# Differential attention in a hybrid encoder layer: the second half of each attention step is queued by a count of TensorE columns

## The chip, the cores and the metric

The kernel runs on one core of a Trainium2 chip. The metric is the device time of one execution in microseconds. Three runs of the kernel before gave 915.10, 917.85 and 918.49 us; the median is 917.85 us. One more execution was recorded by the hardware profiler; that execution took 916.89 us, and the span of its trace, from first to last instruction, is 915.0 us. All durations here come from that trace.

## The reference

One encoder layer over 512 tokens of width 1024, in float32. The part that the change touches is the attention branch: 8 heads, each with two softmax maps over 64-wide queries and keys, and values of 128 columns.

```python
q = apply_rope(rms_norm(q, q_norm_gain[l]), cos, sin)
k = apply_rope(rms_norm(k, k_norm_gain[l]), cos, sin)
# for one block of 128 queries:
s = jnp.einsum('bqhcd,bkhcd->bhcqk', q_blk, k) * scale       # c: the two maps
p = jax.nn.softmax(s, axis=-1)
p_diff = p[:, :, 0] - lam * p[:, :, 1]
o = jnp.einsum('bhqk,bkhd->bqhd', p_diff, v)
# then per head: o = rms_norm(o, attn_subln_gain) * (1 - lam_init), and the output projection
```

Around it stand an RG-LRU branch ahead of attention, the gates and output projections behind it, and a mixture of 16 experts that takes the last third of the time.

## The kernel before, in words

**Precision.** Every large product is made of three: each operand is split into a high part (a cast on ScalarE, L186) and a low part (a subtraction on VectorE, L187), and high x high, high x low and low x high are added in PSUM. So each weight tile that a projection uses costs ScalarE and VectorE one instruction each.

**The attention stage** runs over four pairs of heads (`for j in range(4)`, L735), and in each over eight steps: two heads `hh` times four blocks `t` of 128 queries. A step has three parts:

- `scores` (L617): for each of the two maps two TensorE products of 512 columns into the tile `sps`, a row maximum on VectorE (L630, into `mx`), and an exponential on ScalarE (L631, into `ee`, with the row sum by a second, accumulator-reading instruction).
- `apply_v` (L635): two tiny VectorE instructions on `mx` (L638, L639), then one of 512 columns that makes `ee` the difference of the two maps (L640); four TensorE transposes of `ee` into `pps` (L643); ScalarE casts `pps` to the high part of `PT` (L186), VectorE subtracts to get the low part (L187).
- `outputs` (L647), put into a list `held` by `apply_v`: four products with the high part of `PT` and four with the low part into `ops` (L651), a copy on ScalarE (L653) and an addition on VectorE (L654). After a head's last step, `finish_head` (L660) normalizes the head (L666 to L670) and puts its own transposes, `turn` (L672), into `held`.

**Work beside the steps.** So that TensorE has something to do while ScalarE and VectorE make a step's softmax, chunks of other work are put beside the steps (list `beside`): for pairs 0 to 2 the query/key projections of the next pair (`qk_tok`, four chunks of 24 products of 512 columns, with L559 on ScalarE, L560 to L572 on VectorE and L182, L574, L575 on GpSimd behind each), its value projections (`v_half`, two chunks of 48 products of 256 columns), the stacking of queries and keys (`stack`), and gate chunks of 24 products (`gate_pieces`). Pair 3 has gate chunks only.

**What sets the order.** The Python code gives the program order. `held` is a list of [columns, function]; each projection and each `scores` calls `go_on` (L360) after a group of products, which takes the group's columns off every entry and runs those that reach zero, behind that group on TensorE. On each engine the instructions are then put into a fixed order ahead of time by a scheduler of the language, which keeps program order as priority and lets an instruction pass others where it takes those for not yet ready. On the chip each engine works through its own list in order and waits on semaphores.

In the loop of L753, step `n` first does all but the last of its chunks, then the scores of step `n + 1`, then `apply_v` of step `n`, then its last chunk:

```python
for p_ in beside[n][:-1]: p_()
if n + 1 < len(steps): sm[n + 1] = scores(pr, *steps[n + 1])
apply_v(pr, hh, t, *sm.pop(n))
for p_ in beside[n][-1:]: p_()
```

Of the kernel before, what the change touches and what calls it, by code (L numbers as in the profile page):

```python
# [24 lines left out]
NH = 8  # L25
# [13 lines left out]
BEHIND = 29  # L39
FIRST = 3  # L40
HEAD = 18000
WARM = 20
BETWEEN = (4, 4, 2)
VALUES = 2500
# [58 lines left out]
def _bc(ap, axis, n):  # L103
    a = ap.unsqueeze(axis)
    shape = list(a.shape)
    shape[axis] = n
    return a.broadcast_to(shape)
# [3 lines left out]
def hybrid_layer(ctx, tc, x, w_in, w_ao, w_lo, w_out, w_lg, w_rt, w_eg, w_eu, w_ed, pp, rw, cst, out):  # L111
# [4 lines left out]
    def f(ap):  # L116
        return ap.bitcast(F32)
# [12 lines left out]
    def pss(name):  # L130
        return psp.tile([P, 512], F32, tag="S", name=name, bufs=3)

    def pm(name, dt=F32):
        return psp.tile([P, 512], dt, tag="M", name=name, bufs=3)
# [23 lines left out]
    def unit(tag, shape, dt, name):  # L158
        pool, n = places[tag]
        return pool.tile(shape, dt, tag=tag, name=name, bufs=n)  # L160
# [9 lines left out]
    def keep_busy(n, behind=None):  # L170

        with ExitStack() as order:
            if behind is not None:
                order.enter_context(tc.issue_after(behind))
            for _ in range(n):
                mm(idle_ps, idle[:, 0:P], idle, start=True, stop=True)

    keep_busy(WARM)

    def rpow(dst, src):  # L180
        n = src.free_size()
        return POOL.tensor_tensor(dst, src, mhalf[:, :n], op=ALU.pow)  # L182


    def split(dst_hi, dst_lo, src, eng=DVE):
        i_ = ACT.copy(dst_hi, src)  # L186
        return i_.ins, eng.tensor_tensor(dst_lo, src, f(dst_hi), op=ALU.subtract).ins  # L187
# [167 lines left out]
    held = []  # L355
# [4 lines left out]
    def go_on(last, n):  # L360

        for h in held:
            h[0] -= n
        due = [h for h in held if h[0] <= 0]
        for h in due:
            held.remove(h)
            with tc.issue_after(last.ins):
                h[1]()
# [222 lines left out]
    def stack(pr, hh, qi):  # L591


        j = pr.j
        ps = pm(f"tps{qi}{j}{hh}")
        for t in range(NT):
            PE.transpose(ps[:, t * P:(t + 1) * P], pr.qr[qi][:, t, hh * P:(hh + 1) * P], ident)
        names = ("q",) if qi == 0 else ("k0", "k1")
        st = [unit(n, [P, 2, S], F32R, f"st_{n}{j}{hh}") for n in names]
        for s in range(2):  # L600
            own, oth = slice(64 * s, 64 * s + 64), slice(64 - 64 * s, 128 - 64 * s)
            a = st[0][:, s]
            ACT.copy(a[own], ps[own])
            DVE.tensor_tensor(a[oth], ps[own], f(a[own]), op=ALU.subtract)
            pr.st[hh, qi, s, 0] = a
            if qi:
                b = st[1][:, s]
                ACT.copy(b[oth], ps[own])
                DVE.tensor_copy(b[own], a[oth])
                pr.st[hh, qi, s, 1] = b  # L610

    def new_pair(j):
        pr = Pair()
        pr.j, pr.qr, pr.st, pr.s0s, pr.on = j, {}, {}, {}, {}
        return pr

    def scores(pr, hh, t):  # L617
        h = 2 * pr.j + hh
        if t == 0:
            pr.s0s[hh] = at.tile([P, NT], F32, tag="s0s", name=f"s0s{h}", bufs=2)  # L620
            pr.on[hh] = at.tile([P, NT, P], F32, tag="on", name=f"on{h}", bufs=2)
        mx = at.tile([P, 6], F32, tag="mx", name=f"mx{h}{t}", bufs=3)
        ee = unit("ee", [P, 2, S], F32, f"ee{h}{t}")
        for c in range(2):
            ps = pss(f"sps{h}{t}{c}")
            q = pr.st[hh, 0, c, 0][:, t * P:(t + 1) * P]
            mm(ps, q, pr.st[hh, 1, c, 0], start=True, stop=False)
            l = mm(ps, q, pr.st[hh, 1, c, 1], start=False, stop=True)  # L628
            go_on(l, 2 * 512)
            DVE.tensor_reduce(mx[:, c:c + 1], ps, axis=AX.X, op=ALU.max, negate=True)  # L630
            ACT.activation(ee[:, c], ps, AF.Exp, bias=mx[:, c:c + 1],  # L631
                           accum_out=(pr.s0s[hh][:, t:t + 1] if c == 0 else mx[:, 3:4]))
        return mx, ee

    def apply_v(pr, hh, t, mx, ee):  # L635

        h = 2 * pr.j + hh
        DVE.reciprocal(mx[:, 4:5], mx[:, 3:4])  # L638
        DVE.scalar_tensor_tensor(mx[:, 5:6], pr.s0s[hh][:, t:t + 1], NEGLAM, mx[:, 4:5], op0=ALU.mult, op1=ALU.mult)  # L639
        DVE.scalar_tensor_tensor(ee[:, 0], ee[:, 1], mx[:, 5:6], ee[:, 0], op0=ALU.mult, op1=ALU.add)  # L640
        pt = pm(f"pps{h}{t}")
        for kb in range(NT):
            PE.transpose(pt[:, kb * P:(kb + 1) * P], ee[:, 0, kb * P:(kb + 1) * P], ident)  # L643
        PT = unit("PT", [P, 2, S], F32R, f"PT{h}_{t}")
        split(PT[:, 0], PT[:, 1], pt)

        def outputs():  # L647
            po = pm(f"ops{h}{t}")
            for i in range(2):
                for kb in range(NT):  # L650
                    mm(po[:, 0:256], PT[:, i, kb * P:(kb + 1) * P], pr.vhl[kb // 2][:, kb % 2, hh],  # L651
                       start=(kb == 0 and i == 0), stop=(kb == NT - 1 and i == 1))
            ACT.copy(pr.on[hh][:, t], po[:, P:256])  # L653
            DVE.tensor_tensor(pr.on[hh][:, t], pr.on[hh][:, t], po[:, 0:P], op=ALU.add)  # L654
            if t == NT - 1:
                finish_head(pr, hh)

        held.append([VALUES, outputs])

    def finish_head(pr, hh):  # L660
        h = 2 * pr.j + hh
        on, s0s = pr.on[hh], pr.s0s[hh]
        so = at.tile([P, 3, NT], F32, tag="so", name=f"so{h}", bufs=2)
        sj = at.tile([P, P], BF16, tag="sj", name=f"sj{h}")
        for t in range(NT):
            ACT.activation(sj, on[:, t], AF.Square, accum_out=so[:, 0, t:t + 1])  # L666
        DVE.scalar_tensor_tensor(so[:, 1], s0s, P * EPS, s0s, op0=ALU.mult, op1=ALU.mult)
        DVE.tensor_tensor(so[:, 1], so[:, 1], so[:, 0], op=ALU.add)
        rpow(so[:, 2], so[:, 1])
        POOL.tensor_tensor(on, on, _bc(so[:, 2], 2, P), op=ALU.mult)  # L670

        def turn():  # L672
            pt = pm(f"otp{h}")
            for t in range(NT):
                PE.transpose(pt[:, t * P:(t + 1) * P], on[:, t], ident)
            if pr.j < 3:
                ACT.activation(oT[pr.j][:, hh], pt, AF.Copy, scale=subg)
            else:
                hi, lo = new_o(h)
                ACT.activation(hi, pt, AF.Copy, scale=subg)  # L680
                DVE.scalar_tensor_tensor(lo, pt, subg, f(hi), op0=ALU.mult, op1=ALU.subtract)

        held.append([HEAD, turn])

    oS = {}

    def new_o(h):

        o = unit(("qr", "qr", "va", "vb", "q", "k0", "k1", "ee")[h], [P, 2, S], F32R, f"o{h}")
        oS[h] = o[:, 0], o[:, 1]  # L690
        return oS[h]

    def split_o(h):
        split(*new_o(h), oT[h // 2][:, h % 2])

    def pieces(pr):
        return [lambda t=t: qk_tok(pr, t) for t in range(NT)] + \
               [lambda tp=tp: v_half(pr, tp) for tp in range(2)]
# [16 lines left out]
    pr = new_pair(0)  # L715
# [19 lines left out]
    for j in range(4):  # L735
        nxt = new_pair(j + 1) if j < 3 else None
        beside = [[] for _ in range(2 * NT)]
        beside[0] += [lambda: stack(pr, 1, 0), lambda: stack(pr, 1, 1)]
        if nxt:
            for n, p_ in zip((0, 1, 2, 3, 5, 6), pieces(nxt)):  # L740
                beside[n].append(p_)
            beside[5].append(lambda: stack(nxt, 0, 0))
            beside[6].append(lambda: stack(nxt, 0, 1))
            for n in GATES[j]:
                beside[n].append(gates.pop(0))
        else:
            for n, h in ((2, 0), (2, 1), (3, 2), (4, 3), (5, 4), (6, 5)):
                beside[n].append(lambda h=h: split_o(h))
            for n in GATES[j]:
                beside[n].append(gates.pop(0))  # L750
        steps = [(hh, t) for hh in range(2) for t in range(NT)]
        sm = {0: scores(pr, *steps[0])}
        for n, (hh, t) in enumerate(steps):  # L753
            for p_ in beside[n][:-1]:
                p_()
            if n + 1 < len(steps):
                sm[n + 1] = scores(pr, *steps[n + 1])
            apply_v(pr, hh, t, *sm.pop(n))
            for p_ in beside[n][-1:]:
                p_()  # L760
        pr = nxt


# [115 lines left out]
    pr = pss("rank")  # L879
# [427 lines left out]
```

## Time and profile before

| what | us |
|---|---|
| median of three runs | 917.85 |
| the profiled execution | 916.89 |
| its span | 915.0 |
| TensorE busy in the span | 878.4 |
| VectorE busy | 696.6 |
| ScalarE busy | 589.8 |
| GpSimd busy | 219.1 |
| attention stage, first scores to last chunk | about 255 to 494 in the span |

In the profile, PE is TensorE's products, PEld its weight loads, DVE VectorE, ACT ScalarE, POOL GpSimd. A name such as `sps` is the program's tile without its number; L643 is a line of the kernel. A product of 512 columns is shown with a modelled length of 0.39 us, while such products start 0.23 us apart, so a busy TensorE is judged by starts, not by lengths.

### The profile page before, as it was taken

How to read it: one execution, taken by the hardware profiler on the slowest of the kernel's cores; microseconds unless marked ns; L12 is line 12 of the kernel's file. 1: busy time of each engine (PE TensorE's matmuls, PEld its weight loads, DVE VectorE, ACT ScalarE, POOL GpSimd, SP SyncE). 2: the span in 40 equal slices, each digit the busy share in tenths (PEclk: the TensorE clock that was granted, in tenths of full speed). 3: DMA queues.
4: the chain of work that ended last, by engine and by line, in shares of the span. 5: the costliest groups of instructions: out<-in, count | busy, mean ns of one | idle time of the engine just before them, and what ended most of it. 6: DMA issues, size and time to landing. Idle time of an engine off the chain costs nothing. (4 is left out here: it accounts for less than half of the span.)

```text
span 915.0 us, 12610 instructions
## 1 busy us (share of the span) xinstructions
PE 878.4 (96%) x4504; PEld 700.1 (77%) x4504; DVE 696.6 (76%) x1091; ACT 589.8 (64%) x917; POOL 219.1 (24%) x215
## 2 busy tenths in 40 slices
PE   8999999999999999999999999969999999999993
PEld 5887787788878978878888878947777777777772
DVE  5558977864389689887895653579999999999982
ACT  6698887533255565765784323338888888888881
POOL 6600000080027027056110001432312311121010
PEclk9999999999999999999999999979999999999997
DMA  6621422323312222203236277589999999999952
GB/s 228 211 92 47 138 80 82 93 92 116 92 46 71 51 64 69 70 1 116 93 104 242 92 246 246 179 266 360 364 349 360 377 356 345 371 375 348 384 174 37
DMA packets 50616, 169.92 MB, mean 186 GB/s; under 512 B 6176, under 2 KB 6224, under 8 KB 50544
## 3 DMA queue, kind: packets, MB, share of 16 engines
q1 hardware_dynamic: 43168, 145.77, 45.4%
q0 software_dynamic: 6944, 21.68, 9.2%
q10 hardware_dynamic: 432, 1.57, 0.5%
q8 instruction: 37, 0.61, 0.3%
q14 instruction: 35, 0.29, 0.1%
HBM read 156.94 MB, written 12.06 MB: 185 GB/s over the span
## 5 line engine op out<-in xcount | busy, mean ns | idle before, releaser
L187 DVE TENSOR_TENSOR we_l<-we,we_h 128x1024 fp32r<-128x1024 f32 x128 | 154.2, 1225 | 15.5 <-ACT we_h L186 14.5
L186 ACT CAST we_h<-we 128x1024 fp32r<-128x1024 f32 x128 | 132.6, 1050 | 28.3 <-PE mgu L1131 15.8
L1129 PE MATMUL mgu<-we_h,hx 128*104 128x512 f32 x256 | 102.8, 402 | 0.0
L1130 PE MATMUL mgu<-we_l,hx 128*104 128x512 f32 x256 | 101.5, 397 | 0.1
L1131 PE MATMUL mgu<-we_h,hx 128*104 128x512 f32 x256 | 101.6, 397 | 0.0
L182 POOL TENSOR_TENSOR rk<-ss,mhalf 128x8 f32<-128x8 f32 x16 | 27.3, 1709 | 258.8 <-DVE ss L561 258.8
L186 ACT CAST wd_h<-wd 128x1024 fp32r<-128x1024 f32 x64 | 67.3, 1051 | 21.4 <-PE mgu L1131 20.4
L187 DVE TENSOR_TENSOR wd_l<-wd,wd_h 128x1024 fp32r<-128x1024 f32 x64 | 77.6, 1223 | 2.1 <-ACT wd_h L186 1.9
L630 DVE TENSOR_REDUCE mx<-sps 128x1 f32<-128x512 f32 x64 | 42.7, 684 | 19.3 <-PE sps L628 19.0
L1131 PEld LDWEIGHTS mgu<-we_h,hx 128*104 128x104 f32 x256 | 43.4, 169 | 16.3 <-DVE hx L187 0.2
L1130 PEld LDWEIGHTS mgu<-we_l,hx 128*104 128x104 f32 x256 | 43.5, 170 | 15.4 <-DVE we_l L187 0.3
L1129 PEld LDWEIGHTS mgu<-we_h,hx 128*104 128x104 f32 x256 | 43.4, 170 | 15.2 <-ACT hx L186 0.2
L1129 PE MATMUL py<-wd_h,hh 128*104 128x512 f32 x128 | 52.7, 412 | 0.6 <-ACT hh L186 0.6
L382 PE MATMUL qps<-wqk_l,hT 128*128 128x512 f32 x128 | 50.5, 395 | 1.3 <-DVE wqk_l L187 1.2
L631 ACT ACTIVATE ee<-sps,mx 128x512 f32<-128x512 f32 x64 | 43.8, 689 | 11.0 <-DVE mx L630 10.9
L381 PE MATMUL qps<-wqk_h,hT 128*128 128x512 f32 x128 | 50.9, 399 | 0.0
L231 PE MATMUL gps<-hT,wg_h 128*128 128x512 f32 x128 | 50.4, 394 | 0.0
L383 PE MATMUL qps<-wqk_h,hT 128*128 128x512 f32 x128 | 50.4, 395 | 0.0
L233 PE MATMUL gps<-hT,wg_l 128*128 128x512 f32 x128 | 50.3, 393 | 0.0
L1131 PE MATMUL py<-wd_h,hl 128*104 128x512 f32 x128 | 50.2, 394 | 0.0
L1130 PE MATMUL py<-wd_l,hh 128*104 128x512 f32 x128 | 50.2, 392 | 0.0
L232 PE MATMUL gps<-hT,wg_h 128*128 128x512 f32 x128 | 50.1, 391 | 0.0
(321 smaller groups left out, 2420.2 us busy)
## 6 DMA issues: line engine op xcount, KB each, us to landing
we<-in_w_eg_dram SPq DMA_DIRECT2D x64, 512.0 KB, 10.9
wd<-in_w_ed_dram SPq DMA_DIRECT2D x64, 512.0 KB, 12.8
we<-in_w_eu_dram SPq DMA_DIRECT2D x61, 512.0 KB, 12.8
wg_r<-in_w_in_dram SPq DMA_DIRECT2D x16, 512.0 KB, 3.9
wqk_r<-in_w_in_dram SPq DMA_DIRECT2D x16, 512.0 KB, 5.0
wlo_r<-in_w_lo_dram SPq DMA_DIRECT2D x8, 512.0 KB, 3.9
wv_r<-in_w_in_dram SPq DMA_DIRECT2D x8, 512.0 KB, 3.7
wao_r<-in_w_ao_dram SPq DMA_DIRECT2D x8, 512.0 KB, 4.3
```

Of the source, the lines that this page charges most:

```text
L186: i_ = ACT.copy(dst_hi, src)
L187: return i_.ins, eng.tensor_tensor(dst_lo, src, f(dst_hi), op=ALU.subtract).ins
L231: mm(ps, wh, ah, start=first, stop=False)
L232: mm(ps, wh, al, start=False, stop=False)
L233: return mm(ps, wl, ah, start=False, stop=last)
L381: mm(ps, a, w[0][k], start=(k == 0), stop=False)
L382: mm(ps, a, w[1][k], start=False, stop=False)
L383: go_on(mm(ps, b, w[0][k], start=False, stop=(k == KD - 1)), 3 * 512)
L631: ACT.activation(ee[:, c], ps, AF.Exp, bias=mx[:, c:c + 1], accum_out=(pr.s0s[hh][:, t:t + 1] if c == 0 else mx[:, 3:4]))
L1129: mm(ps, ah, wh, start=first, stop=False)
L1130: mm(ps, ah, wl, start=False, stop=False)
L1131: last_mm[0] = mm(ps, al, wh, start=False, stop=last).ins
```

## The change

A constant `EXPS = 6000` is added. `scores` of a step now puts that step's `apply_v` into `held`, to be run when 6000 columns of products have been issued behind the scores. If that has not happened by the end of the step's own pass through the loop, it is run there. The chunk that came behind `apply_v` now comes behind the next step's scores directly. The last head's `turn` is queued with 18000 - 6000 columns instead of 18000.

```diff
+EXPS = 6000
...
-        held.append([HEAD, turn])
+        held.append([HEAD - (EXPS if h == NH - 1 else 0), turn])
...
-        sm = {0: scores(pr, *steps[0])}
+        waits = {}
+
+        def score(n):
+
+            hh, t = steps[n]
+            sm = scores(pr, hh, t)
+            waits[n] = [EXPS, lambda pr=pr: apply_v(pr, hh, t, *sm)]
+            held.append(waits[n])
+
+        score(0)
         for n, (hh, t) in enumerate(steps):
             for p_ in beside[n][:-1]:
                 p_()
             if n + 1 < len(steps):
-                sm[n + 1] = scores(pr, *steps[n + 1])
-            apply_v(pr, hh, t, *sm.pop(n))
+                score(n + 1)
             for p_ in beside[n][-1:]:
                 p_()
+            if any(h is waits[n] for h in held):
+                held[:] = [h for h in held if h is not waits[n]]
+                waits[n][1]()
```

Instructions and transfers are the same in number; SyncE's queue keeps its order but for one swap of two neighbouring weight loads. TensorE, VectorE, ScalarE and GpSimd have theirs reordered through the whole attention stage. Line numbers of the changed kernel are one higher up to the loop, twelve higher behind it.

**TensorE, pair 0, around the transposes of the third step** (`pps`; `sps` are scores, `qps` the query/key projection, `ops` the outputs). Before:

```order
L382 MATMUL qps_2248<-wqk_l_2168,hT_112 128x512
L383 MATMUL qps_2248<-wqk_h_2167,hT_113 128x512
L627 MATMUL sps_2302<-st_k_1823,st_q_1813 128x512
L628 MATMUL sps_2302<-st_k_1824,st_q_1813 128x512
L627 MATMUL sps_2307<-st_k_1823,st_q_1813 128x512
L628 MATMUL sps_2307<-st_k_1824,st_q_1813 128x512
L643 MATMUL pps_2315<-cst_sb,ee_2226 128x128 x4
L381 MATMUL qps_2323<-wqk_h_2149,hT_112 128x512
```

And now:

```order
L383 MATMUL qps_2259<-wqk_l_2157,hT_112 128x512
L644 MATMUL pps_2275<-cst_sb,ee_2248 128x128 x4
L384 MATMUL qps_2259<-wqk_h_2156,hT_113 128x512
L628 MATMUL sps_2324<-st_k_1823,st_q_1813 128x512
L629 MATMUL sps_2324<-st_k_1824,st_q_1813 128x512
L628 MATMUL sps_2329<-st_k_1823,st_q_1813 128x512
L652 MATMUL ops_2289<-vhl_1845,PT_2_2280 128x256 x2
L652 MATMUL ops_2289<-vhl_1961,PT_2_2280 128x256 x2
L629 MATMUL sps_2329<-st_k_1824,st_q_1813 128x512
```

The transposes stood behind the next step's four score products; now they stand ahead of them, before the last product of the chunk, and the first products with `PT` follow four products later.

**VectorE at the same place**, from the row maxima of a step to its `ee`. Before:

```order
L630 TENSOR_REDUCE mx_2300<-sps_2302 128x1
L560 TENSOR_REDUCE ss_2285<-sq_2284 128x8
L568 TENSOR_TENSOR qr_2171<-qps_2248,rope 128x256
L561 TENSOR_SCALAR ss_2285<-ss_2285 128x8
L568 TENSOR_TENSOR qr_2172<-qps_2248,rope 128x256
L572 TENSOR_TENSOR t_2289<-qps_2248,rope 128x8x32 x2
L630 TENSOR_REDUCE mx_2300<-sps_2307 128x1
L187 TENSOR_TENSOR PT_2_2320<-pps_2315,PT_2_2320 128x512
L667 SCALAR_TENSOR_TENSOR so_2418<-s0s_2085 128x4
L638 RECIPROCAL mx_2300<-mx_2300 128x1
L639 SCALAR_TENSOR_TENSOR mx_2300<-s0s_2085,ls,mx_2300 128x1
L640 SCALAR_TENSOR_TENSOR ee_2301<-ee_2301,mx_2300 128x512
```

And now:

```order
L188 TENSOR_TENSOR PT_2_2280<-pps_2275,PT_2_2280 128x512
L561 TENSOR_REDUCE ss_2307<-sq_2306 128x8
L569 TENSOR_TENSOR qr_2160<-qps_2259,rope 128x256
L562 TENSOR_SCALAR ss_2307<-ss_2307 128x8
L569 TENSOR_TENSOR qr_2161<-qps_2259,rope 128x256
L655 TENSOR_TENSOR on_2086<-on_2086,ops_2289 128x128
L573 TENSOR_TENSOR t_2311<-qps_2259,rope 128x8x32 x2
L631 TENSOR_REDUCE mx_2322<-sps_2324 128x1
L631 TENSOR_REDUCE mx_2322<-sps_2329 128x1
L668 SCALAR_TENSOR_TENSOR so_2375<-s0s_2085 128x4
L639 RECIPROCAL mx_2322<-mx_2322 128x1
L640 SCALAR_TENSOR_TENSOR mx_2322<-s0s_2085,ls,mx_2322 128x1
```

The low part of `PT` and the whole work behind a projection chunk now stand ahead of both row maxima; the row that makes `ee` follows next. Before, the first row maximum stood ahead of that work.

**VectorE at the start of pair 0**, the first two steps. Now:

```order
L639 RECIPROCAL mx_2087<-mx_2087 128x1
L639 RECIPROCAL mx_2124<-mx_2124 128x1
L610 COPY st_k_2115<-st_k_2114 64x512
L640 SCALAR_TENSOR_TENSOR mx_2087<-s0s_2085,ls,mx_2087 128x1
L640 SCALAR_TENSOR_TENSOR mx_2124<-s0s_2085,ls,mx_2124 128x1
L641 SCALAR_TENSOR_TENSOR ee_2088<-ee_2088,mx_2087 128x512
L641 SCALAR_TENSOR_TENSOR ee_2125<-ee_2125,mx_2124 128x512
```

Both steps are now done in one go, the second step's two small instructions ahead of the first step's `ee`; before, they stood behind it.

## Rows read from the trace of the kernel before

**Rows 1.** The page: busy us, share of the span and instructions of each engine.

```profile
PE 878.4 (96%) x4504; PEld 700.1 (77%) x4504; DVE 696.6 (76%) x1091; ACT 589.8 (64%) x917; POOL 219.1 (24%) x215
```

**Rows 2.** Windows of 40 us: busy time by engine, then PEclk, DMA share, GB/s.

```profile
260.00:300.00 40.00, 38.90 (x206) 31.58 (x205) 34.36 (x71) 21.70 (x51) 24.25 (x22) 1.00 0.24 66
...
sum 240.00, PE 235.32 PEld 198.18 DVE 197.22 ACT 150.70 POOL 85.65; mean PE 39.22 PEld 33.03 DVE 32.87 ACT 25.12 POOL 14.27
```

**Rows 3.** All waits of PE, 240 to 520 us: us, times, longest us.

```profile
PE pps L643 <- DVE ee L640: 2.9, 7, 1.0
PE pps L643 <- DVE mx L638: 0.9, 2, 0.5
PE ops L651 <- DVE PT L187: 0.8, 4, 0.2
```

**Rows 4.** Timeline, first step of pair 0 (start, length, engine, line).

```profile
262.92 0.39 PE L628 MATMUL sps<-st_k,st_q 128*128 128x512 f32 x1
263.15 0.40 PE L627 MATMUL sps<-st_k,st_q 128*128 128x512 f32 x1
263.24 0.75 DVE L640 SCALAR_TENSOR_TENSOR ee<-ee,mx 128x512 f32<-128x512 f32 x1
263.91 0.15 DVE L638 RECIPROCAL mx<-mx 128x1 f32<-128x1 f32 x1
264.05 0.66 PE L643 MATMUL pps<-cst_sb,ee 128*128 128x128 f32 x4 [0.50 <-DVE ee L640]
264.46 0.48 PE L628 MATMUL sps<-st_k,st_q 128*128 128x512 f32 x1
264.74 0.59 ACT L186 CAST PT<-pps 128x512 fp32r<-128x512 f32 x1 [1.00 <-PE pps L643]
265.47 0.65 PE L651 MATMUL ops<-vhl,PT 128*128 128x256 f32 x4
```

**Rows 5.** Timeline, second to fourth step of pair 0, a step's chain.

```profile
270.22 0.63 PE L643 MATMUL pps<-cst_sb,ee 128*128 128x128 f32 x4 [0.36 <-DVE mx L638]
270.88 0.59 ACT L186 CAST PT<-pps 128x512 fp32r<-128x512 f32 x1 [1.74 <-PE pps L643]
271.59 0.68 DVE L187 TENSOR_TENSOR PT<-pps,PT 128x512 fp32r<-128x512 f32 x1
274.02 0.69 DVE L630 TENSOR_REDUCE mx<-sps 128x1 f32<-128x512 f32 x1 [0.34 <-PE sps L628]
274.29 0.60 PE L643 MATMUL pps<-cst_sb,ee 128*128 128x128 f32 x4
274.63 0.68 DVE L560 TENSOR_REDUCE ss<-sq 128x8 f32<-128x512 f32 x1
276.62 0.68 DVE L630 TENSOR_REDUCE mx<-sps 128x1 f32<-128x512 f32 x1
277.22 0.68 DVE L187 TENSOR_TENSOR PT<-pps,PT 128x512 fp32r<-128x512 f32 x1
278.15 0.16 DVE L638 RECIPROCAL mx<-mx 128x1 f32<-128x1 f32 x1
278.80 1.64 POOL L575 TENSOR_TENSOR qr<-qr,rk 128x256 f32<-128x256 f32 x2
278.91 1.07 DVE L640 SCALAR_TENSOR_TENSOR ee<-ee,mx 128x512 f32<-128x512 f32 x1
282.19 0.60 PE L643 MATMUL pps<-cst_sb,ee 128*128 128x128 f32 x4
```

**Rows 6.** Timeline, seventh step of pair 0, beside a value chunk.

```profile
307.95 0.16 DVE L638 RECIPROCAL mx<-mx 128x1 f32<-128x1 f32 x1
308.15 0.22 DVE L639 SCALAR_TENSOR_TENSOR mx<-s0s,ls,mx 128x1 f32<-128x1 f32 x1
308.41 0.75 DVE L640 SCALAR_TENSOR_TENSOR ee<-ee,mx 128x512 f32<-128x512 f32 x1
```

**Rows 7.** L640 alone: duration in ns, min/median/max.

```profile
L640 DVE SCALAR_TENSOR_TENSOR ee<-ee,mx x32: 732/751/1192, 263.2 to 488.0; 128x512 f32<-128x512 f32 x32
```

## The prediction, made before the changed kernel ran

> **What bounds the kernel now.** I read the busy times first. TensorE is busy for 878.4 us, 96% of the span, and no other compute engine is above 76% [rows 1], so an order can gain only what TensorE idles in the stage that it changes. The windows of that stage say how much this is: over 240 us TensorE is busy for 235.32, at full clock in the window shown, and VectorE for 197.22, in the first window 34.36 of 40 [rows 2]. VectorE has little room in these windows, though it is not the bound. Then the waits of TensorE in the stage: transposes of `ee` for VectorE, 2.9 us in 7 waits and 0.9 us in 2, and products with the low part of `PT`, 0.8 us in 4 [rows 3]. That is all: 4.6 us in 13 waits.
>
> The timeline shows that a wait costs a little more than its idle time. Two score products start 0.23 us apart (262.92, 263.15); the transposes that should follow at 263.38 start at 264.05, 0.67 us late, where the row shows 0.50 idle, since the modelled length covers the first 0.17 [rows 4]. With 0.17 for each of the 13, the stage loses 4.6 + 2.2 = 6.8 us. This is the ceiling of the gain: 916.9 - 6.8 = 910.1 us.
>
> **What the change moves.** No instruction is added or removed, so every term is a wait on TensorE. SyncE's queue has one swap of neighbours, and the expert weights that it loads there have the projections behind attention to arrive in: zero. The last head's `turn` still comes behind the same number of products: zero. GpSimd's list is shuffled within the stage; it works 85.65 of 240 us [rows 2] and TensorE waits nowhere for it [rows 3]: zero by itself.
>
> What matters is the new place of the transposes. By columns, 6000 behind the scores would be in the middle of a chunk. The order shows most of them much later, at the last or the last but one product of a chunk, or right behind the scores of a later step. The scheduler puts an instruction at its counted place unless it takes it for not ready; so a transpose that stands later stands where the scheduler expected `ee` to be just ready. Before, many transposes stood behind the next step's scores, with time in hand: in the third and fourth step of pair 0 VectorE had ended `ee` 2.2 us and more ahead of the transposes (278.91 + 1.07 = 279.98 against 282.19 [rows 5]). That cover is gone now, so I work out the chain that ends in `ee`.
>
> **A steady step** (transposes at the end of a query/key chunk; 6 of the 32 steps stand there). Call the start of one step's transposes T and follow VectorE's new order to the next step's `ee`, with the starts of the same instructions as measured. Transposes to cast 0.66, cast to the low part of `PT` 0.71 (270.22, 270.88, 271.59): T+1.37. That instruction holds VectorE for 0.60 (as the maximum at 274.02 does the next, 274.63): L560 at T+1.97. From L560 to the maximum L630 it was 274.63 to 276.62, 1.99 us; `outputs`' addition is now in between, which I estimate at 0.29 (the 0.68 of an instruction on four times the elements bounds it from above, 0 from below): first maximum at T+4.25, second 0.61 later at T+4.86. From the second maximum to L640 2.29 (276.62, 278.91), with a `PT` row of 0.6 between which ScalarE's exponential covered anyway; L640 takes 1.07, and 0.06 passes to the transposes (263.99, 264.05 [rows 4]): T+8.28. TensorE's own work between two such transposes is 282.19 - 274.29 = 7.90 us [rows 5], and stays that. So each steady step is late by 0.38 us. Both ends: where GpSimd isn't at work, L638 to the end of L640 takes 1.21 (307.95 to 309.16 [rows 6]) instead of 1.83, and the chain, at T+7.66, is hidden: 0. The longest L640 is 1.19 us [rows 7]; that gives 0.50. I take 0.38, since GpSimd's L575 follows the projection chunk in every such step, as at 278.80: 6 x 0.38 = 2.3 us over the stage.
>
> The Trainium skill (SBUF — State Buffer, "Who interferes with whom") says that a VectorE instruction with two SBUF inputs, which L640 is, waits for a GpSimd instruction that reads SBUF until that one has finished. The trace agrees that they disturb each other (0.75 alone, 1.07 beside L575) but not with a full block: two L575 take 1.64, so L640 behind the first would end at 278.80 + 0.82 + 0.75 = 280.37 and not at 279.98. By the rule each steady step would lose 0.4 us more, the sum would be 2.3 us higher.
>
> **The start of a pair.** In pair 0 the two first steps are now done together. Two small instructions (0.15 and 0.22 [rows 4, 6]) stand ahead of the first `ee`, so the transposes start at 264.05 + 0.37 = 264.42; TensorE gets there one score later than before, 263.61: lost 0.81. The second `ee` ends 0.67 later (263.24, 263.91), 0.41 for the transposes (264.05, 264.46) and one product lie between: nothing more than 0.1. The first products with `PT` stand right behind; they need the cast, which ends 0.69 + 0.59 behind the transposes, and start 1.42 behind them at the earliest (264.05, 265.47 [rows 4]): at 265.84, while TensorE is free at about 265.5: lost 0.35. Together about 1.3. Before, the two steps cost 0.67 and 0.36 + 0.17 (270.22 [rows 5]), 1.2. So the early work wins nothing here.
>
> **The sum.** Pair 0 after: 1.3 for the start, 3 x 0.38 for the steady steps, 0.4 for the step beside the gate chunk (weight splits stand on VectorE ahead of its `ee`; sized by the steady step, ends 0 and 0.8), 2 x 0.2 beside the value chunks (there no query/key work is on VectorE; ends 0 and 0.4), and 2 x 0.1 for the first products with `PT`, which now come 0.41 + 4 x 0.23 = 1.33 us behind the transposes and need 1.42. That is 3.4 us. In pairs 1 and 2 one transpose each stands in the middle of its chunk, at its counted place, and has time in hand: 3.0 each. Pair 3, with no query/key work on VectorE, had almost no waits and is left with 0.3. After: 3.4 + 6.0 + 0.3 = 9.7 us, before 6.8, so +2.9, and the profiled execution's 916.9 would become 919.8. The median of the runs is 1.0 higher than that execution; on it the same sum gives 920.8. I predict 920.5.
>
> **Rivals.**
> - *The waits go and no new ones come.* If `ee` is really ready where the scheduler expects it, TensorE runs through. For it: with every `apply_v` issued early, VectorE does a step's `ee` as soon as it can. Against: all 9 waits on `pps` [rows 3] stand where the scheduler had moved the transposes by that same expectation. Two thirds of the 6.8 us gone: 912.5.
> - *Every moved transpose waits as those did.* The mechanism is TensorE held at `pps` in nearly each of the 24 steps of pairs 0 to 2, not only at some: mean wait (2.9 + 0.9)/9 = 0.42, with 0.17 0.59 us. 24 x 0.59 = 14.2, with 1.4 for `PT` and 0.3 for pair 3 15.9, less 6.8: +9.1, 926.0. It decides as soon as the chain is longer than 8.2 us also beside value and gate chunks. Against it: VectorE has pauses there.
> - *It cancels.* The new waits are as many as the old: 917 to 918.5. The order of pair 0's start, with the same 1.3 us on either side, speaks for it.
>
> **How the numbers follow.** The forecast 0.42, the first rival 0.22, the second 0.22, the third 0.14. About 0.5%, 4.6 us, is what a measurement of this kernel can tell from no change: below 913.3 is faster, above 922.4 slower. The first rival is below 913.3 for three quarters of its chance: 0.17 faster. The second is slower altogether, and of the forecast's 0.42 a third lies above 922.4, where the quiet end of the steady step doesn't come: 0.36 slower. The rest, 0.47, is within. The range goes from 912.5, the first rival's number, to 926.5, just past the second's; the forecast's own is 917.5 to 923.5.
>
> **What would show it.** Right: in the stage the row of TensorE waiting at `pps` for `ee` grows from 9 waits to 15 or more, of 0.2 to 0.6 us each, the steady steps are 8.1 to 8.5 us apart instead of 7.90, and the busy times outside the stage don't move. Wrong: fewer than 9 such waits, or transposes with `ee` ready over 1 us ahead in the steady steps. If the end moves with the stage unchanged, the cause lies behind it, in the loads of the expert weights, and the whole sum is beside the point.

## The result and the profile after

The changed kernel takes 923.06 us (median of 7 runs, 920.56 to 924.65), the kernel before, beside it, 917.54 us (915.10 to 918.49). The ratio is 1.006, with a 95% interval of 1.0042 to 1.0078: the change costs about 5.5 us. 920.5 was forecast, so the direction and the place were right and the size was short by half. The profiled execution of the changed kernel took 923.06 us with a span of 921.1.

The page's busy times first; the line answers to [rows 1].

```profile
span 921.1 us, 12621 instructions
...
PE 879.8 (96%) x4504; PEld 700.3 (76%) x4504; DVE 698.0 (76%) x1091; ACT 589.3 (64%) x917; POOL 215.8 (23%) x215
```

No engine has more work: TensorE's busy time grew by 1.4 us, the span by 6.1. The windows of the attention stage say the same (answers to [rows 2]): TensorE is busy 3.4 us less in the same 240 us.

```profile
sum 240.00, PE 231.89 PEld 194.66 DVE 196.88 ACT 149.20 POOL 80.99; mean PE 38.65 PEld 32.44 DVE 32.81 ACT 24.87 POOL 13.50
```

The waits of TensorE in the stage, the answer to [rows 3] (us in total, times, longest):

```profile
PE pps L644 <- DVE ee L641: 5.1, 9, 1.1
PE pps L644 <- DVE mx L639: 1.4, 1, 1.4
PE ops L652 <- DVE PT L188: 0.8, 1, 0.8
PE otp L676 <- POOL on L671: 0.7, 3, 0.3
PE sps L628 <- ACT ee L632: 0.2, 1, 0.2
```

4.6 us have become 8.2, and the transposes alone 3.8 have become 6.5, in ten waits instead of nine: hardly more waits, but longer ones. From the first score product to the first product of the projection behind attention it is 244.2 us instead of 239.4, 4.9 us more. Counted by starts, where a product of 512 columns is given 0.23 us until the next start, one of 256 columns 0.12 and one of 128 columns 0.11, the transposes are late by 10.4 us in that time, before by 6.7. So 3.7 of the 4.9 us stand ahead of transposes. Of the rest, score products start 1.3 us later in sum and the transposes of finished heads 0.8, while other starts win back 0.9; no run shows why the score products are late. Outside the stage it is 676.9 against 675.6 us. The profiled runs of the experiments lie between 674.2 and 676.2 there and scatter by more than this 1.3 us, so it is not put down to the change.

One of the longest waits, on VectorE, GpSimd and TensorE, beside the first gate and value chunks of pair 0 (start, length, engine, line):

```profile
293.70 1.31 DVE L188 TENSOR_TENSOR wv_l<-wv_r,wv_h 128x1024 fp32r<-128x1024 f32 x1
293.89 1.71 POOL L575 TENSOR_TENSOR qr<-qr,t 128x256 f32<-128x256 f32 x1
294.93 0.15 DVE L639 RECIPROCAL mx<-mx 128x1 f32<-128x1 f32 x1
295.00 1.68 DVE L188 TENSOR_TENSOR wv_l<-wv_r,wv_h 128x1024 fp32r<-128x1024 f32 x1
295.56 1.59 POOL L576 TENSOR_TENSOR qr<-qr,rk 128x256 f32<-128x256 f32 x1
296.61 0.57 DVE L640 SCALAR_TENSOR_TENSOR mx<-s0s,ls,mx 128x1 f32<-128x1 f32 x1
297.12 0.61 POOL L576 TENSOR_TENSOR qr<-qr,rk 128x256 f32<-128x256 f32 x1
297.21 1.07 DVE L641 SCALAR_TENSOR_TENSOR ee<-ee,mx 128x512 f32<-128x512 f32 x1
298.42 0.63 PE L644 MATMUL pps<-cst_sb,ee 128*128 128x128 f32 x4 [0.91 <-DVE ee L641]
```

Read it from the bottom. The transposes wait 0.91 us for `ee`. `ee` is late since three VectorE instructions ahead of it ran while GpSimd worked on the rotated queries: the second weight split took 1.68 us, the one-column row L640 0.57 and L641, which makes `ee`, 1.07, where the same instructions alone take 1.22, 0.22 and 0.75. That is 1.1 us, about the wait. The two engines take turns here: each of the three began while a GpSimd row was at work, and ended 1.08, 0.03 and 0.55 us behind the end of that row (295.60, 297.15, 297.73).

### The profile page after: what moved, and what is told of

The parts are those of the page before. It is cut to its first block, busy times and chain, and to the rows that moved or that the text cites. A ratio compares the mean times of both kernels' runs of the same rounds, so it can differ in the third digit from the quotient of the medians.

```text
span 921.1 us, 12621 instructions
## 1 busy us (share of the span) xinstructions
PE 879.8 (96%) x4504; PEld 700.3 (76%) x4504; DVE 698.0 (76%) x1091; ACT 589.3 (64%) x917; POOL 215.8 (23%) x215
## 5 line engine op out<-in xcount | busy, mean ns | idle before, releaser
L188 DVE TENSOR_TENSOR we_l<-we,we_h 128x1024 fp32r<-128x1024 f32 x128 | 154.2, 1225 | 15.5 <-ACT we_h L187 14.2
L188 DVE TENSOR_TENSOR wd_l<-wd,wd_h 128x1024 fp32r<-128x1024 f32 x64 | 77.6, 1223 | 2.1 <-ACT wd_h L187 1.7
L631 DVE TENSOR_REDUCE mx<-sps 128x1 f32<-128x512 f32 x64 | 42.6, 684 | 10.4 <-PE sps L629 10.0
## 6 DMA issues: line engine op xcount, KB each, us to landing
we<-in_w_eg_dram SPq DMA_DIRECT2D x64, 512.0 KB, 10.4
```

## The experiments

Theory A: the transposes lost their cover, and stand on TensorE where the scheduler takes `ee` for just ready; B: VectorE's collisions with GpSimd cost the time wherever the transposes stand; C: the count of 6000 is simply too high. Each run was timed beside the kernel before, which had a median of 916.5 us in these series.

**The count of columns.** Four kernels change the count; the last step of the last head keeps its 6000, so that the end of the stage stays as it is.

```diff
-EXPS = 6000
+EXPS = 3000        # and 14336, 17000, 20000
+LAST = 6000
...
-            waits[n] = [EXPS, lambda pr=pr: apply_v(pr, hh, t, *sm)]
+            waits[n] = [LAST if pr.j == 3 and n == 7 else EXPS, lambda pr=pr: apply_v(pr, hh, t, *sm)]
```

3000: 

> The changed kernel with 3000 columns instead of 6000 (the last step of the last head keeps 6000). Theory A, lost cover: the transposes stand where the scheduler takes `ee` for just ready, the count of columns no longer decides, so halving it moves little: 922 to 925 us, 9 to 13 waits of TensorE on `pps`, 6 to 8 us idle. Theory B, GpSimd's collisions with VectorE decide and the place of the transposes doesn't: also 922 to 925. Theory C, the count itself was only tuned wrong towards late: a smaller count gives `PT` earlier and wins back 2 us or more, 918 to 921.

14336: 

> 14336 columns: one chunk of 12288 and the next step's scores of 2048, about the place that the transposes had before, but by the new code. Theory A: the cover is back, 916 to 919 us, waits on `pps` 3 to 5 us. Theory B (collisions of VectorE and GpSimd, whatever the place): 920 to 923. Theory C: worse than the changed kernel, above 924.

17000: 

> 17000 columns: the transposes come some six products behind the next step's scores. Theory A: more cover than the kernel before, the waits on `pps` fall under its 3.8 us: 913 to 917 us. Theory B: 920 to 923. Theory C: above 924.

20000: 

> 20000 columns: the transposes come twelve products, half a chunk, behind the next step's scores. Theory A: waits on `pps` nearly gone, 912 to 917 us; if a new wait takes over, it is the next scores waiting for a free buffer of `ee`. Theory B: 920 to 923. Theory C: above 924.

| columns | median us | ratio to before, 95% interval | stage us | waits on `pps`, us |
|---|---|---|---|---|
| 3000 | 920.35 | 1.0041 (1.0027 to 1.0056) | 242.5 | 4.1 |
| 6000 (the change) | 923.06 | 1.006 (1.0042 to 1.0078) | 244.2 | 6.5 |
| 14336 | 916.83 | 1.0007 (0.9989 to 1.0025) | 239.2 | 3.2 |
| 17000 | 916.46 | 0.9991 (0.9976 to 1.0005) | 238.2 | 2.3 |
| 20000 | 916.65 | 1.0009 (0.9998 to 1.0021) | 239.4 | 2.9 |
| before | 916.5 | 1 | 239.4 | 3.8 |

Theory A holds for the three later places: they bring the whole loss back, with the same code and the same instructions. B in its strong form (920 to 923 at any place) falls, and so does C, which had the later counts above 924. For 3000 columns A was off: it gave 922 to 925 us with 6 to 8 us of waits, and the run shows 920.35 us and 4.1 us. This time lies in the range that C gave, but its interval overlaps that of 6000, so whether the smaller count wins anything is not settled.

Two counts over the traces bear A out. In the kernel before, 12 of the 32 transposes start more than 1 us behind the end of their `ee`; in the changed kernel none does, and with 14336, 17000 and 20000 columns it is 14, 16 and 16. And VectorE lost no more time beside GpSimd than before: in the stage the one-column row ahead of `ee`, the row that makes `ee` and the weight splits exceed the longest that they take with GpSimd idle (0.22, 0.76 and 1.23 us) by 8.1 us in all and by 8.3 before; with 17000 columns it is 6.5 and with 20000 it is 9.2, and neither loses time. No run moved the transposes alone, since VectorE's order changes with the count. With 17000 the third and fourth step's transposes of pair 0 have no wait any more:

```profile
274.26 0.60 PE L645 MATMUL pps<-cst_sb,ee 128*128 128x128 f32 x4
282.09 0.60 PE L645 MATMUL pps<-cst_sb,ee 128*128 128x128 f32 x4
```

and the stage is left with these waits:

```profile
PE pps L645 <- DVE ee L642: 2.3, 6, 0.6
PE ops L653 <- DVE PT L189: 0.3, 1, 0.3
PE otp L677 <- POOL on L672: 0.3, 1, 0.3
```

Of the 2.3 us for `ee` 1.6 stand at the first or the last step of a pair; the longest wait, 0.6, stands at the third step of pair 2. The hope for 913 to 917 came out at its upper end. With 20000 columns the waits were to be nearly gone; 2.9 us of them are left, and the time is no better than with 17000. No count beats the kernel before beyond the measurement: the interval of 17000 reaches from 2.2 us faster to 0.5 us slower.

**Without GpSimd's part of the query/key chunks.** From the kernel before and from the changed one four GpSimd instructions per query/key chunk are left out: the second half of the rotation is not added and the heads are not scaled. GpSimd's other rows, among them the scaling of a finished head (L671 in the changed kernel), stay: 151 of 215 instructions.

```diff
-        for qi in range(2):
-            POOL.tensor_tensor(r3[qi], r3[qi], t2t[:, qi], op=ALU.add)
-            POOL.tensor_tensor(r3[qi], r3[qi], _bc(rs_[:, 4 * qi:4 * qi + 4], 2, 64), op=ALU.mult)
```

In the kernel before: 

> The kernel before with GpSimd's four instructions behind a query/key chunk left out (the rotated half is not added and the scaling is missing), so that GpSimd can't slow VectorE there. Both theories: a base for the next run; 913 to 917 us, waits on `pps` for VectorE 1.5 to 3.8 us.

In the changed kernel: 

> The changed kernel with the same four instructions left out; the transposes stand at the same places in the order. Theory A1 (cover lost; what makes `ee` late is VectorE slowed beside GpSimd, which the scheduler doesn't foresee): the waits on `pps` fall from 6.5 to under 3 us and the kernel is within 2 us of the run without the change, 914 to 918. Theory A2 (cover lost; the chain through ScalarE and VectorE is too long by itself): waits stay at 5 to 7 us, 4 to 6 us slower than the run without the change, 918 to 922.

Before without it: 914.34 us (ratio to the kernel before 0.9972, 0.996 to 0.9984), waits on `pps` 2.4 us. Changed without it: 917.61 us (1.001, 0.9996 to 1.0025). The waits of the latter:

```profile
PE pps L641 <- DVE ee L638: 1.8, 8, 0.3
PE pps L641 <- DVE mx L636: 1.4, 1, 1.4
PE otp L673 <- POOL on L668: 0.3, 1, 0.3
PE sps L625 <- ACT ee L629: 0.2, 1, 0.2
```

Nine waits for `ee` of up to 1.1 us have become eight of up to 0.3. The order of the other engines is all but the same: by the names in the traces VectorE and ScalarE work through the same rows in the same order, and TensorE's list differs at 8 of 4504 places. So GpSimd sets the size of these waits. The two times differ by 3.3 us in the medians and the two stages by 2.5 us, where the change costs 5.5 and 4.9 us with all of GpSimd at work. So the answer lies between A1 and A2: about half of the loss goes with these four instructions, by a sum whose ends overlap. A1 had asked for waits under 3 us and a difference within 2 us; it is 3.2 and 3.3.

What is left is not free of GpSimd. The 1.4 us stand at the start of pair 1, where VectorE makes the stacks of the second head ahead of the first `mx`, and there a cast of these stacks runs beside the scaling that stays (L671, here L668):

```profile
326.11 1.04 POOL L668 TENSOR_TENSOR on<-on,so 128x512 f32<-128x512 f32 x1
326.31 1.12 DVE L607 CAST st_k<-st_k 64x512 fp32r<-64x512 f32 x1
```

Elsewhere in this trace the cast takes 0.42 us, so by an estimate from these rows up to 0.7 of the 1.4 us belong to it. Four of the eight waits for `ee`, 1.0 us together, also stand behind a one-column row of 0.60 to 0.99 us beside the same scaling. No run leaves that scaling out, so how much of the loss would stay without any of GpSimd's work is open.

That GpSimd lengthens VectorE's rows shows in their durations. The first fence is of the kernel before, the second of the changed kernel, the third of the changed one without the four GpSimd instructions (durations in ns, min/median/max, then first and last start):

```profile
L187 DVE TENSOR_TENSOR wv_l<-wv_r,wv_h x8: 1211/1222/1608, 207.5 to 421.6; 128x1024 fp32r<-128x1024 f32 x8
```

```profile
L188 DVE TENSOR_TENSOR wv_l<-wv_r,wv_h x8: 1215/1464/1767, 207.0 to 426.1; 128x1024 fp32r<-128x1024 f32 x8
L631 DVE TENSOR_REDUCE mx<-sps x64: 671/683/694, 254.5 to 492.0; 128x1 f32<-128x512 f32 x64
```

```profile
L188 DVE TENSOR_TENSOR wv_l<-wv_r,wv_h x8: 1205/1214/1225, 207.0 to 420.4; 128x1024 fp32r<-128x1024 f32 x8
L638 DVE SCALAR_TENSOR_TENSOR ee<-ee,mx x32: 732/751/754, 262.6 to 488.2; 128x512 f32<-128x512 f32 x32
```

The change moved the value splits into GpSimd's time, their median rose from 1222 to 1464 ns; without the four instructions they and `ee` never take longer than alone (`ee` up to 754 ns, against 1192 in [rows 7]).

**Which steps.** 6000 columns for some steps, 17000 for the others.

```diff
+LATE = 17000
...
+            waits[n] = [LAST if pr.j == 3 and n == 7 else EXPS if pr.j < 3 and n in (2, 3, 4) else LATE, ...]
```

Early for the third to fifth step of pairs 0 to 2: 

> 6000 columns only for the third, fourth and fifth step of pairs 0 to 2 (the steady steps of the prediction), 17000 for the rest. By the prediction's term these cost 0.38 us each for six: 2.3 us over the run with 17000 everywhere (916.5), so 918 to 920. By the trace of the changed kernel, in which these steps of pair 0 have no wait and those of pair 2 have 0.8 each: 1 to 2 us, 917 to 918.5.

The reverse, with `EXPS` and `LATE` exchanged in the condition: 

> The reverse: 17000 columns for those three steps of pairs 0 to 2, 6000 for the rest, among them the steps with weight splits on VectorE. By the prediction's sum the rest costs little: 917 to 919. By the trace of the changed kernel, whose longest waits stand beside weight splits and at the start of pairs: 919 to 922.

The first gives 919.0 us (1.0031, 1.0018 to 1.0045), in the range of the prediction's term and above that of the trace; the second gives 917.21 us (1.0009, 0.9995 to 1.0023). Over the run with 17000 everywhere the nine steps cost 2.5 us, by the ratios 0.0040 or 3.7 us, and the rest 0.8, by the ratios 1.7. So the nine steps seem to cost more than the rest, though the two intervals overlap a little. By the ratios the two add up to 0.9991 + 0.0040 + 0.0018 = 1.0049, inside the interval of the whole change. By the stages of the traces they do not: 2.4 and 1.5 us (240.6 and 239.7 against 238.2), together 3.9, where the whole change has 6.0. So some 2 us may come only when both are early, and no run shows why. The second run fell below what the changed kernel's trace had led me to expect (919 to 922): waits that stand beside a weight split in one order need not stand there in the next.

The waits of the first of them show how the cost of these steps is made up:

```profile
PE pps L646 <- DVE ee L643: 3.1, 9, 0.8
PE ops L654 <- DVE PT L190: 1.8, 4, 0.7
PE otp L678 <- POOL on L673: 0.3, 1, 0.3
```

Over the run with 17000 everywhere the transposes wait 0.8 us more and the products with the low part of `PT` 1.5 us more. They follow closely behind the transposes now, as the rows of the order show, and in three of the four cases VectorE comes to the subtraction only behind two weight splits.

## Why the prediction was right, and where it was not

**What bounds.** Right in the main: the loss is in the stage, and three quarters of it stand ahead of the transposes, 3.7 us where the whole sum had 2.9. The 1.3 us of later score products had no term in the sum. TensorE's granted clock is 1.00 in each of the six windows of the stage, before and after, and with the later counts nothing of the loss is left, so no run shows a part for the other stages.

**The lost cover.** Right, and it is what the counts show: the same transposes behind the next scores cost nothing. That the scheduler's own expectation of `ee` sets their new places was argued and is not shown by itself; what is shown is that none of the 32 has 1 us in hand any more.

**A steady step: 0.38 us, six of them 2.3 us.** The sum is near what the run with nine steps early cost (2.5 us, by the ratios 3.7), but that is luck, since the working did not come true. (The final sum also counts seven such steps, three in pair 0 and two each in pairs 1 and 2, where the term has six.) In pair 0 of the changed kernel the chain was shorter than worked out, as these rows show (the chain of [rows 5], from one step's transposes to the next's):

```profile
272.13 0.60 PE L644 MATMUL pps<-cst_sb,ee 128*128 128x128 f32 x4
272.77 0.59 ACT L187 CAST PT<-pps 128x512 fp32r<-128x512 f32 x1 [2.10 <-PE pps L644]
273.39 0.69 DVE L188 TENSOR_TENSOR PT<-pps,PT 128x512 fp32r<-128x512 f32 x1 [1.49 <-ACT PT L187]
274.00 0.68 DVE L561 TENSOR_REDUCE ss<-sq 128x8 f32<-128x512 f32 x1
276.18 1.28 DVE L631 TENSOR_REDUCE mx<-sps 128x1 f32<-128x512 f32 x2
278.58 0.22 DVE L640 SCALAR_TENSOR_TENSOR mx<-s0s,ls,mx 128x1 f32<-128x1 f32 x1
278.84 1.07 DVE L641 SCALAR_TENSOR_TENSOR ee<-ee,mx 128x512 f32<-128x512 f32 x1
280.05 0.52 PE L644 MATMUL pps<-cst_sb,ee 128*128 128x128 f32 x3
```

From T = 272.13: the low part of `PT` at T+1.26 (worked out 1.37), the first maximum at T+4.05 (4.25), `ee` done at T+7.78 (8.22). It just makes it. The part that was too long is the one from the second maximum to the row that makes `ee` (L640, now L641): 2.06 us instead of 2.29, where the one-column row ahead of it took 0.22 and not 0.53; and two earlier parts were each 0.1 us shorter. In pair 2 the chain was as long as feared and longer, where a weight split stands in it as well:

```profile
415.60 1.23 DVE L188 TENSOR_TENSOR wg_l<-wg_r,wg_h 128x1024 fp32r<-128x1024 f32 x1 [0.21 <-ACT wg_h L187]
415.91 1.82 POOL L671 TENSOR_TENSOR on<-on,so 128x512 f32<-128x512 f32 x1
417.14 0.60 DVE L640 SCALAR_TENSOR_TENSOR mx<-s0s,ls,mx 128x1 f32<-128x1 f32 x1
417.69 0.74 POOL L575 TENSOR_TENSOR qr<-qr,t 128x256 f32<-128x256 f32 x1
417.78 1.20 DVE L641 SCALAR_TENSOR_TENSOR ee<-ee,mx 128x512 f32<-128x512 f32 x1
418.90 1.75 DVE L188 TENSOR_TENSOR wg_l<-wg_r,wg_h 128x1024 fp32r<-128x1024 f32 x1
419.12 0.63 PE L644 MATMUL pps<-cst_sb,ee 128*128 128x128 f32 x4 [0.79 <-DVE ee L641]
420.56 1.63 DVE L188 TENSOR_TENSOR wv_l<-wv_r,wv_h 128x1024 fp32r<-128x1024 f32 x1
422.12 0.68 DVE L188 TENSOR_TENSOR PT<-pps,PT 128x512 fp32r<-128x512 f32 x1
422.86 0.74 PE L652 MATMUL ops<-vhl,PT 128*128 128x256 f32 x4 [0.77 <-DVE PT L188]
```

The wait is 0.79 us for `ee`, where L640 and L641 took 0.60 and 1.20 us beside L671 and L575, and then 0.77 for the low part of `PT`, which stands on VectorE behind splits of 1.75 and 1.63 us.

**The step beside the gate chunk: 0.4 us (ends 0 and 0.8).** Mis-sized, and out of its bounds: the rows of 298.42 above show 0.91 idle, and pair 1 has 1.15 at the same place. The term was taken over from the steady step, with nothing for the two splits; in the rows above the second split and the two rows behind it lost 1.1 us beside GpSimd. In the run of the changed kernel without the four GpSimd instructions this step of pair 0 has no wait, and that of pair 1 0.2 us.

**The products with `PT`: 2 x 0.1 us per pair.** Near in size, wrong in place: no wait in the steady steps of pair 0, one of 0.77 in pair 2, and four of together 1.8 when only the nine steps are early. The working had VectorE reach the subtraction at once.

**The start of a pair: 1.3 us after, 1.2 before.** Nearly right for pair 0, where the first transposes wait 0.48 (263.75) and the second not at all. In pair 1 the wait of 1.0 us before grew to 1.4, where a cast is held up beside GpSimd's L671 as shown above.

**The signs.** Fifteen or more waits of 0.2 to 0.6 us were named as the sign of being right; there are ten on `pps`, of 0.2 to 1.4, so this sign did not come, and the time lies in the range with fewer and longer waits. The periods of the steady steps, 8.1 to 8.5 us, are met only by some: 7.92 and 8.08 in pair 0, 9.1 and 8.09 in pair 1, 9.5 in pair 2 (409.61 to 419.12). Of the rivals, "every moved transpose waits" was wrong in the number of the waits, ten and not 24, and too low in their size, 0.42 us against 0.65.

**GpSimd and VectorE.** The Trainium skill (SBUF — State Buffer, "Who interferes with whom") says that a VectorE instruction with two SBUF inputs contends with a GpSimd instruction that reads SBUF, that one with at most one SBUF input, outside the 2-port perf modes, does not, and that the shared ports are an exclusive lock. The traces agree: L631, which reads PSUM alone, stays at 671 to 694 ns in all 64 executions, while L640, L641 and L188's weight splits are stretched. They agree with the lock too, which the prediction denied. In the ten traces the row that makes `ee` began 73 times while GpSimd's L575, L576 or L671 (the changed kernel's lines) was at work; each time it ended, within 0.02 us, at the later of two moments, 0.75 us behind its own start or 0.55 us behind the end of the GpSimd instruction. In the 21 executions that began before the GpSimd instruction it took at most 0.75 us. So the later one waits. The prediction took each of two L575 as 0.82 us and so missed this; taken singly, the first was shorter:

```profile
278.80 0.62 POOL L575 TENSOR_TENSOR qr<-qr,rk 128x256 f32<-128x256 f32 x1
```

It ended at 279.42, and 0.55 us more is 279.97, where L640 ended at 279.98 [rows 5]. The lock thus asks for the 1.07 us that the sum already had, and not for 0.4 us more per step.

## What to carry to other kernels

Here the change cost time since a consumer on the engine that bounds the kernel was moved to just behind its producer. Before such a move, read from the trace how much time the consumer has in hand now, and keep it where the engine that makes the input is itself nearly full, as VectorE is here (196.88 of 240 us). And a VectorE row that shares time with GpSimd should be counted from the end of the GpSimd instruction that is at work when it begins, not at its median length.

## What was not expected of the hardware

A VectorE instruction of one column (L639 before, L640 now) takes at most 0.22 us in the 193 executions of the ten traces in which GpSimd is idle; in the changed kernel it takes up to 0.77 us beside GpSimd's L575 and L576, and 1.00 beside L671. A weight split takes 1.22 us and up to 1.77, with 2.06 in two of the experiments. Leaving out four GpSimd instructions per chunk, which TensorE hardly ever waits for, made the kernel before 0.28% faster (0.16 to 0.4%).
